# A hybrid decoder layer in split float32: the down projection and the last gate go token-major, half of their columns partly by Strassen's scheme

## The chip, the cores and the metric

The kernel runs on one core of one Trainium2 chip. The metric is the device time of one execution in microseconds (us). Before the change the median of three runs is 1440.21 us (1440.0 to 1440.61). The profile is one further execution of the same program; its first instruction and its last lie 1438.4 us apart (the span).

## The reference: what is computed

One layer over 256 tokens of width 2048, all in float32:

```
u  = rmsnorm(h);  proj = u @ w_in            # q, k, v of 16 heads and two gates
ya = dilated_mixture_attention(...) @ w_branch_a
yb = stick_breaking_attention(...) @ w_branch_b
h  = h + rmsnorm((sigmoid(ga) * ya + sigmoid(gb) * yb) @ w_out, g_mix_post)
u  = rmsnorm(h, g_ffn_pre)
up = causal_depthwise_conv(u @ w_up, conv_w, conv_b)       # 2 x 5632 columns
f  = (gelu(gate_ff) * value) @ w_down                       # 5632 -> 2048
h  = h + rmsnorm(f, g_ffn_post)
e  = p @ w_ple_in
h  = h + sigmoid(h @ w_ple_gate) * e
```

The change touches the last five lines from the product with `w_down` on, and where `h` and `e` are kept.

## The kernel before, in words

**Precision.** TensorE takes its operands as float32r, a rounded float32. Each operand x is therefore kept as two rounded parts, hi = round(x) and lo = round(x - hi), and each product is made of three: hi hi, hi lo and lo hi. For the weights ACT makes hi (L200) and DVE makes lo (L237) from the raw tile that a DMA brought.

**The weight stream.** The list `_plan()` gives the order in which blocks of 128 x 128 weights are used. Eight blocks make an item of 128 x 1024, 512 KB. There are 5 raw buffers (`NRAW`) and 7 pairs of split buffers (`NSPL`). `block()` hands PE the next block; at each eighth it calls `tick`, which writes the work of the other engines into their queues: first the ACT part of the deferred jobs that are due, then the hi of items up to six ahead, then DVE's lo of items that got their hi at an earlier tick, then the DVE part of the deferred jobs. `defer` hands in a job as a list of stages, and at each tick one more job starts and each running one goes on by a stage. Every engine works through its queue in the written order. Loads stand in SP's queue and are written by `lows` as raw buffers come free.

**Two ways to multiply.** By channel (`mul`, L318 and L320): the weights are the stationary operand and the activations the moving one; per block one matmul of 512 columns (hi against hi and lo of 256 tokens) and one of 256 columns (lo against hi), and the result stands with channels on the partitions. A last column group uses three of 256 (`mul1`, L338 to L340), so that no separate addition is left. By token (`three_wide`, L881, and `by_token`, L799 to L801): 128 tokens of the activation are stationary and 512 weight columns move, three matmuls for a half of the tokens, and the result stands with tokens on the partitions.

**Strassen's scheme before the change.** It is in use in `gate_groups` for the two gates of the first sub-layer, three column groups of four: the 2 x 2 blocks are token halves by k-tile pairs by two halves of 512 columns; seven products P1 to P7 take the place of eight. The sums of activation blocks are made once (`combine`), the sums of weight blocks (`weight_sums`, L210 and L211) for each group: the first in DRAM-to-SBUF transfers, a plain one and two that accumulate (`add_ahead`, issued by POOL, L224), the others on DVE. Such a pair of k-tiles is four items in the stream, of which two are sums.

**Residual and channel mixer.** `h` is kept by channel (`gh`). `turn` makes the post-norm of the mixer, adds to `h`, makes `u2`, and has the first half of `e` multiplied meanwhile (PE works on `e` while the norm's chain of small steps runs on DVE and ACT). Then come four quarters (`NQ`): 22 column tiles of `w_up` each (`up_evac`: two PSUM halves added, times the norm factor, the conv, gelu, product, split into `ft`), then 16 column tiles of `w_down` over the quarter's 11 rows of k-tiles, each added into `ff` (L379, L1170). After the last quarter a second `turn` makes the norm of `ff` (a ones-matmul sums squares over the partitions, L1035), the last `h` and its split `u3`, with the second half of `e`; then 16 column tiles of `w_ple_gate`, each with a sigmoid (L1194), a product with `e`, the addition of `h`, and a store of 128 KB.

Of the kernel before, what the change touches and what calls it, by code (L numbers as in the profile page):

```python
# [34 lines left out]
PAIRS = 4  # L35
SETTLE = dict(even=8, turned=9)
# [9 lines left out]
def _plan():  # L46
# [5 lines left out]
    def add(key, cols, nk, runs=None):  # L52
        plan.append((key, cols, runs or [list(range(nk))]))

# [15 lines left out]
    for j in range(0, KT, 4):  # L70
        gates = [[("w_in", o + kind * KT + n) for n in range(j, j + 4)] for kind in range(2)]
        if j == 0:
            add(("ga", j), gates[0], KT, single)
            add(("gb", j), gates[1], KT, single)
        else:

            order = [(4 * kind + c, k) for p in range(PAIRS) for kind, k in ((0, p), (1, p + 8), (0, p + 8), (1, p))
                     for c in range(4)]
            order += [(c, k) for k in _plain() for c in range(8)]
            plan.append((("gates", j), gates[0] + gates[1], order))  # L80
        add(("ba", j), [("w_branch_a", n) for n in range(j, j + 4)], NS, single[:NS])
        add(("bb", j), [("w_branch_b", n) for n in range(j, j + 4)], NS, single[:NS])
# [3 lines left out]
    add(("e", 0), [("w_ple_in", j) for j in range(8)], 2)  # L86
    up = [("w_up", half * NFF + n) for n in range(NFF) for half in range(2)]
    add("up", up[:FIRST], KT, single)
    for q in range(NQ):
# [3 lines left out]
        add(("down", q), [("w_down", j) for j in range(3)], 0, [rows[:-2], rows[-2:-1], rows[-1:]])  # L93
        for j in range(3, KT):
            add(("down", q, j), [("w_down", j)], 0, [rows])
    add(("e", 1), [("w_ple_in", j) for j in range(8, 16)], 2)
    add("pg", [("w_ple_gate", j) for j in range(FIRST)], KT, single)
    for j in range(FIRST, KT):
        add(("pg", j), [("w_ple_gate", j)], KT)
    return plan  # L100

# [13 lines left out]
def hybrid_block_kernel(ctx: ExitStack, tc: tile.TileContext, head, gx, pT, convp, bias, masks, w, out):  # L115
# [20 lines left out]
    stream, used, sums_of = [], 0, {}  # L136
    for g in _plan():
        if g[0][0] == "gates":
            assert used % 8 == 0
            while len(stream) < used // 8 + 2 * len(sums_of):  # L140
                stream.append(len(stream) - 2 * len(sums_of))
            for _ in range(PAIRS):
                i, r = len(stream), len(stream) - 2 * len(sums_of)
                stream += [r, None, None, r + 1]
                sums_of[i] = i + 3
        used += len(_order(g))
# [4 lines left out]
    part = {b for b in sums_of.values()}  # L151
    place = {r: i for i, r in enumerate(stream) if r is not None}
# [10 lines left out]
    def load(i, a=0, b=1024):  # L163
        if i not in raw:
# [5 lines left out]
    for g in _plan():  # L170
        if g[0][0] == "e":
            assert first_block % 8 == 0
            lent += [place[first_block // 8], place[first_block // 8 + 1]]
# [28 lines left out]
    def weight_sums(i):  # L202
# [4 lines left out]
        if n == 1:  # L207
            x = mps["mp"].tile([128, 2, 512], F32, name="wsum")
            raw[i] = [x[:, 0], x[:, 1]]
            DVE.tensor_tensor(x[:, 0], raw[a + 1][0], w0[:, 512:], OP.add)  # L210
            DVE.tensor_tensor(x[:, 1], x[:, 0], w1[:, :512], OP.add)  # L211
        return raw[i]

    def add_ahead(*ms):


        firsts = sorted(sums_of)
        for m in ms:
            if m < len(firsts):
                i, k = firsts[m], (4, 12, 0, 8)[m % PAIRS]  # L220
                to = gh[:, G + k * T:G + (k + 4) * T]
                nc.sync.dma_start(to, w[stream[i] - NE])
                for c in (0, 512):
                    nc.gpsimd.dma_start(to[:, c:c + 512], w[stream[i] + 1 - NE][:, 512:], accum_op=OP.add)  # L224
                raw[i + 1] = [to[:, :512], to[:, 512:]]

    def low(i, a=0, b=1024, src=None):
        if i in sums:
# [3 lines left out]
            if sums[i][1]:  # L232
                add_ahead(sorted(sums_of).index(sums[i][0]) + PAIRS)
# [122 lines left out]
    def mm(key, src, fn=mul, ps=None, even=0, turned=None, mid=None):  # L356
# [4 lines left out]
        for n, (_, k, first, last) in enumerate(group(key)):  # L361
            if n == 3 and mid:
                mid()
# [27 lines left out]
    gh = keep.tile([128, 4 * KT + KT * T], F32, name="gh")  # L391
# [491 lines left out]
    def gate_groups(j, merged):  # L883
# [3 lines left out]
        P3 = pm.tile([128, 2 * T], F32, name="sum")  # L887
# [52 lines left out]
    for j in range(0, KT, 4):  # L940
        if j:
            ga, gb = gate_groups(j, merged)
        else:
            for kind in ("ga", "gb"):
# [3 lines left out]
                if kind == "ga":  # L948
# [5 lines left out]
                    banks["of"] = [(pm1, 4), (pm, 3)] * 3 + [(pm1, 4)]  # L954
# [69 lines left out]
    def turn(half, edst, src, gnext, dst, nxt):  # L1024
# [3 lines left out]
        pr = pm.tile([128, 2 * T], F32, name="sum")  # L1028
        pse = []
        for i, (n, k, first, last) in enumerate(group(("e", half))):  # L1030
            if n % 2 == 0 and first:
                pse.append(bank())
            mul1(pse[-1][:, n % 2 * T:(n % 2 + 1) * T], pTs[:, k], first and n % 2 == 0, last)
            if i == 3 + half:
                PE.matmul(pr[:, :T], f(ones), sq[:, 0], start=True, stop=True)  # L1035
        rstd(pr)
        pss = [bank() for _ in range(FIRST)]
        gn = [None if gnext is None else gain(gnext, k) for k in range(KT)]
# [22 lines left out]
        def keep_e(n):  # L1061
            ACT.activation(edst[:, 2 * n:2 * n + 2].rearrange("p a b -> p (a b)"), pse[n], AF.Copy)
# [18 lines left out]
        for c, k, first, last in group(nxt):  # L1081
# [18 lines left out]

    e0 = fp.tile([128, 8, T], F32, name="e0")
    pss = turn(0, e0, mix, 2, u2, "up")


    ff = keep.tile([128, KT, T], F32, name="ff", tag="acc")
    ft = fp.tile([128, QT, 2 * T], F32R, name="ft", tag="ft")
    cpad = [fp.tile([128, T + 2], F32, name=f"cpad{n}") for n in range(4)]
    for c in cpad:
        DVE.memset(c[:, 0:2], 0.0)
    conv = {}  # L1110

    def up_evac(n, ps):

        c = cpad[n % 4]
# [17 lines left out]
        if n % 2:  # L1132
            st.append((lambda: usplit(ft, t, a, low=False), lambda: ulow(ft, t, a)))
        defer(*st)

    keys = [("up", n) for n in range(2 * NFF)]
    def mid():
        total(pm.tile([128, 2 * T], F32, name="sum"), sp)
# [8 lines left out]
    for n in range(FIRST, FIRST + 2):  # L1147
        pss.append(mm(keys[n], u2))
    flush()
    sp = halves()  # L1150
    for q in range(NQ):
        for n in range(max(len(pss), q * 2 * QT), (q + 1) * 2 * QT):
            ps = mm(keys[n], u2, **dict(SETTLE, mid=mid) if n == len(pss) else {})
            up_evac(n, ps)
        if q == NQ - 1:
            u3 = keep.tile([128, KT, 2 * T], F32R, name="u3", tag="u")
            lend(1, u3)
        down = several(("down", q), 3, ft)
        if q == NQ - 1:
            ACT.preload_act_table_set(LNEXP)  # L1160
        for j in range(KT):
            if q == NQ - 1 and j == KT - 1:
                break
            ps = down[j] if j < 3 else mm(("down", q, j), ft)

            def then(sum_to, j=j, q=q):
                if q == 0:
                    sum_to(ff[:, j])
                else:
                    DVE.tensor_tensor(ff[:, j], ff[:, j], sum_to(temp()), OP.add)  # L1170
            defer(both(ps, then), *([squares(ff, j), scaled(ff, j, 3)] if q == NQ - 1 else []))
    ps = mm(("down", NQ - 1, KT - 1), ft, mul1)
    lows(at["high"])
    flush()
    DVE.tensor_tensor(ff[:, KT - 1], ff[:, KT - 1], ps[:, :T], OP.add)
    square_sum(ff[:, KT - 1])
    scaled(ff, KT - 1, 3)[0]()


    e1 = fp.tile([128, 8, T], F32, name="e1", tag="ft")  # L1180
    pss = turn(1, e1, ff, None, u3, "pg")
    ACT.preload_act_table(AF.Sigmoid)

    def pg_evac(j, ps, whole=False):
        s = temp()
        e = (e0 if j < 8 else e1)[:, j % 8]
        first = (None, None) if whole else both(ps, lambda sum_to: sum_to(s))

        def dve():
            DVE.tensor_tensor(s, s, e, OP.mult)  # L1190
            o = temp("t", 3)
            DVE.tensor_tensor(o, s, h[:, j], OP.add)
# [81 lines left out]
```

## Time and profile before

| what | value |
|---|---|
| median of three runs | 1440.21 us |
| range | 1440.0 to 1440.61 us |
| span of the profiled execution | 1438.4 us |
| time of a run outside the span (median less span) | 1.8 us |
| PE busy | 1433.0 us, 100% of the span |
| DVE busy | 1086.7 us, 76% |
| ACT busy | 839.4 us, 58% |
| DMA | 290.78 MB, mean 202 GB/s |

The stage boundaries, from the first matmul of each stage: first half of `e` at 599.3 us, `up` from 605.5 us, the four stretches of `down` from 728.1, 911.1, 1094.2 and 1277.2 us, the second half of `e` at 1338.4 us, the gate `pg` from 1344.5 us; the last matmul starts at 1433.8 us. A matmul's duration in the profile is longer than its distance to the next one, since matmuls overlap in the array: rates are read from stretches of time and counts, not from the mean duration.

### The profile page before, as it was taken

How to read it: one execution, taken by the hardware profiler on the slowest of the kernel's cores; microseconds unless marked ns; L12 is line 12 of the kernel's file. 1: busy time of each engine (PE TensorE's matmuls, PEld its weight loads, DVE VectorE, ACT ScalarE, POOL GpSimd, SP SyncE). 2: the span in 40 equal slices, each digit the busy share in tenths (PEclk: the TensorE clock that was granted, in tenths of full speed). 3: DMA queues.
4: the chain of work that ended last, by engine and by line, in shares of the span. 5: the costliest groups of instructions: out<-in, count | busy, mean ns of one | idle time of the engine just before them, and what ended most of it. 6: DMA issues, size and time to landing. Idle time of an engine off the chain costs nothing.

```text
span 1438.4 us, 21464 instructions
## 1 busy us (share of the span) xinstructions
PE 1433.0 (100%) x8052; PEld 1254.9 (87%) x8052; DVE 1086.7 (76%) x1645; ACT 839.4 (58%) x1282; POOL 21.7 (2%) x29
## 2 busy tenths in 40 slices
PE   9999999999999999999999999999999999999998
PEld 8888888888888888988888888888888888888987
DVE  7876666669889865799965788767887677878784
ACT  7665555566556655576654555545655455657562
POOL 0000000002110000000000000000000000000000
PEclk9999999999999999999999999999999999999999
DMA  7754746479986776555766566666566666667381
GB/s 283 270 169 160 248 146 214 146 251 271 315 256 226 251 235 204 175 167 186 230 190 189 186 192 189 194 189 188 189 191 191 192 188 192 189 191 213 109 271 51
DMA packets 83334, 290.78 MB, mean 202 GB/s; under 512 B 9248, under 2 KB 11680, under 8 KB 83104
## 3 DMA queue, kind: packets, MB, share of 16 engines
q1 hardware_dynamic: 79776, 283.13, 61.4%
q0 software_dynamic: 3456, 6.29, 2.5%
q8 instruction: 63, 1.03, 0.3%
q14 instruction: 39, 0.32, 0.1%
HBM read 287.29 MB, written 2.10 MB: 201 GB/s over the span
## 4 chain that ended last, share of the span: by engine, by line
PE 100%; DVE 0%; ACT 0%; issue 0%
PE mm L318 47%; PE mm L320 24%; PE mm L881 7%; PE mm L646 2%; PE mm L644 2%; PE mm L645 2%; PE mm L799 2%; PE mm L800 2%; PE mm L801 2%; PE sum L881 2%; PE mm L340 1%; PE mm L339 1%; PE mm L338 1%; PE S L318 0%; PE S L657 0%; PE po L657 0%
## 5 line engine op out<-in xcount | busy, mean ns | idle before, releaser
L237 DVE TENSOR_TENSOR lo<-raw,hi 128x1024 fp32r<-128x1024 f32 (+1 forms) x497 | 596.5, 1210 | 155.2 <-ACT hi L200 149.2
L318 PE MATMUL mm<-u,hi 128*128 128x512 f32 x2044 | 710.4, 392 | 0.0
L200 ACT ACTIVATE hi<-raw 128x1024 fp32r<-128x1024 f32 (+1 forms) x497 | 516.0, 1046 | 227.5 <-PE mm L318 163.2
L320 PE MATMUL mm<-u,lo 128*128 128x256 f32 x2032 | 569.1, 280 | 0.0
L318 PEld LDWEIGHTS mm<-u,hi 128*128 128x128 f32 x2044 | 381.6, 187 | 82.5
L320 PEld LDWEIGHTS mm<-u,lo 128*128 128x128 f32 x2032 | 384.0, 189 | 1.3 <-DVE lo L237 0.6
L318 PE MATMUL mm<-ft,hi 128*128 128x512 f32 x693 | 240.4, 391 | 0.0
L376 ACT ACTIVATE t<-mm 128x256 f32<-128x256 f32 x209 | 79.0, 378 | 197.3 <-PE mm L320 197.0
L320 PE MATMUL mm<-ft,lo 128*128 128x256 f32 x693 | 194.0, 280 | 0.0
L318 PEld LDWEIGHTS mm<-ft,hi 128*128 128x128 f32 x693 | 129.6, 187 | 28.4
L379 DVE TENSOR_TENSOR s<-mm,t 128x256 f32<-128x256 f32 x178 | 75.1, 422 | 96.2 <-ACT t L376 96.2
L320 PEld LDWEIGHTS mm<-ft,lo 128*128 128x128 f32 x693 | 131.0, 189 | 0.0
L318 PE MATMUL mm<-mg,hi 128*128 128x512 f32 x232 | 80.5, 392 | 0.0
L881 PE MATMUL mm<-hi,u 128*128 128x512 f32 x192 | 66.2, 391 | 0.0
L320 PE MATMUL mm<-mg,lo 128*128 128x256 f32 x230 | 64.4, 280 | 0.0
L1123 ACT ACTIVATE cv<-cpad,cw 128x256 f32<-128x256 f32 x88 | 52.7, 599 | 8.1 <-DVE cpad L1118 7.8
L318 PEld LDWEIGHTS mm<-mg,hi 128*128 128x128 f32 x232 | 43.3, 187 | 9.3
L644 PE MATMUL mm<-hi,u 128*128 128x512 f32 x128 | 50.9, 398 | 0.0
L646 PE MATMUL mm<-hi,u 128*128 128x512 f32 x128 | 50.0, 391 | 0.0
L645 PE MATMUL mm<-lo,u 128*128 128x512 f32 x128 | 49.9, 390 | 0.0
L1127 DVE SCALAR_TENSOR_TENSOR cv<-cpad,cw,cv 128x256 f32<-128x256 f32 x88 | 42.7, 485 | 3.1
L320 PEld LDWEIGHTS mm<-mg,lo 128*128 128x128 f32 x230 | 43.5, 189 | 0.1
(287 smaller groups left out, 1548.0 us busy)
## 6 DMA issues: line engine op xcount, KB each, us to landing
raw<-in_w SPq DMA_DIRECT2D x501, 512.0 KB, 3.6
gh<-in_w SPq DMA_DIRECT2D x12, 512.0 KB, 5.3
gh<-in_w POOLq DMA_DIRECT2D x24, 256.0 KB, 7.6
hd<-in_head SPq DMA_DIRECT2D x6, 576.0 KB, 8.1
gh<-in_gx SPq DMA_DIRECT2D x6, 512.0 KB, 4.7
bi<-in_bias SPq DMA_DIRECT2D x4, 576.0 KB, 4.7
out<-t SPq DMA_DIRECT2D x16, 128.0 KB, 3.8
gh<-in_gx SPq DMA_DIRECT2D x1, 1056.0 KB, 7.5
```

The source lines that it names most:

```text
L200: ACT.activation(hi[i][:, a:b], raw[i][:, a:b] if src is None else src, AF.Copy)
L237: DVE.tensor_tensor(lo[i][:, a:b], raw[i][:, a:b] if src is None else src, f(hi[i][:, a:b]), OP.subtract)
L318: PE.matmul(ps, wh, rhs, start=first, stop=last, skip_group_check=True)
L320: PE.matmul(ps[:, :T], wl, rhs[:, :T], start=False, stop=last, skip_group_check=True)
L376: ACT.activation(t1[0], ps[:, T:], AF.Copy)
L379: DVE.tensor_tensor(out, ps[:, :T], t1[0], OP.add)
L644: PE.matmul(pv[t], xh, wh, start=kt == 0, stop=False)
L645: PE.matmul(pv[t], xh, wl, start=False, stop=False)
L646: PE.matmul(pv[t], xl, wh, start=False, stop=kt == KT - 1)
L881: PE.matmul(ps, x[i], w[j], start=first and n == 0, stop=last and n == 2, skip_group_check=True)
L1123: ACT.activation(y, c[:, 2:], AF.Identity, scale=cw[:, n, 2:3], bias=cw[:, n, 3:4])
L1127: DVE.scalar_tensor_tensor(y, c[:, 0:T], cw[:, n, 0:1], y, op0=OP.mult, op1=OP.add)
```

## The change

`w_down` and `w_ple_gate` are multiplied by token. Of the 16 column tiles, eight (1024 columns) take part of their rows by Strassen's scheme: in `down` eight of the eleven rows of a quarter in four pairs, in `pg` eight of sixteen k-tiles in four pairs; the rest of these columns' rows is plain, and the other eight column tiles are two groups `four` of 512 columns. The first weight sum of pairs 0 and 3 is made by transfers ahead of time (`sum_early`), the other sums on DVE; for pairs with transferred sums only half of the second weight tile is loaded. The activation sums of the pairs (`parts`) are made in `up_evac`. `join` and `join_to` put the seven products together, `ends` adds the plain rows.

The residual goes to token order: `home` transposes `h` in four calls of eight transposes among the first `up` tiles into `hx`. The norm of `ff` then needs no ones-matmul: squares are summed along the free axis (`square_to`), and the gain comes as a full tile (`weigh`). `turn_back` transposes the new `h` to channel order in eight calls of four, for `u3`. Since `hx` takes its space, the first half of `e` goes to DRAM and comes back before `pg`. `e` is made by token in four groups, and the output is stored by token in larger pieces. Eight PSUM banks now form one ring of 4 + 4; the separate bank `sum` is gone.

```diff
+DROWS = 8
+DSUM = (0, 3)
...
+        plan.append((("pairs", "down", q), down[:8],
+                     paired([(rows[r], rows[r + 1]) for r in range(0, DROWS, 2)]) + whole(rows[DROWS:])))
+        for c in (8, 12):
+            add(("down", q, c), down[c:c + 4], 0, [[r] for r in rows])
...
+    add(("pg", 0), pg[:4], KT, single)
+    plan.append((("pairs", "pg"), pg[4:12],
+                 whole(range(2 * PAIRS, KT)) + paired([(2 * p, 2 * p + 1) for p in range(PAIRS)])))
+    add(("pg", 12), pg[12:], KT, single)
...
+            if n == 0 or a in by_dma:
+                x = mps["mp"].tile([128, 2, 512], F32, name="wsum", tag="wsum")
...
+            if n == 0:
+                DVE.tensor_tensor(x[0], w0[:, :512], w1[:, 512:], OP.add)
+                DVE.tensor_tensor(x[1], w0[:, 512:], w1[:, 512:], OP.add)
+            else:
+                DVE.tensor_tensor(x[0], raw[a + 1][0], w0[:, 512:], OP.add)
+                DVE.tensor_tensor(x[1], x[0], w1[:, :512], OP.add)
...
+        def sums():
+            y.append(tmp.tile([128, 4, H], F32, name="y4", tag="s2", bufs=2))
+            DVE.tensor_tensor(y[0][:, 0], k1[:, H:], k2[:, H:], OP.subtract)
...
+        for p, (k1, k2) in enumerate(pairs):
+            last = p == len(pairs) - 1
+            s = [[mixed[:, p, i, n] for i in range(2)] for n in range(4)]
+            w11, w22 = item()
+            add(1, cut(src, k1, 0), w11, last)
+            if last:
+                ACT.activation(p1_to, bk[1], AF.Copy)
+            add((0, 1), s[3], w22, last and first_plain)
+            q, t3 = item()
+            add(5, s[0], q, last)
+            add(7, s[2], t3, last)
+            t2, t4 = item()
+            add(6, s[1], t2, last)
+            add((1, 0), cut(src, k2, 1), t4, last and first_plain)
+            w21, _ = item()
+            add((0, 0), cut(src, k2, 0), w21, last and first_plain)
...
-        pss.append(mm(keys[n], u2))
+        pss.append(mm(keys[n], u2, mid={3: home(8 * (n - FIRST)), 11: home(8 * (n - FIRST) + 4)}))
...
+    for t in range(2):
+        to = ff[:, t, 3 * 512:]
+        DVE.tensor_tensor(to, to, ps[t], OP.add)
+        square_to(t, 3)
+        ACT.activation(ln[:, t], ss[:, t, 3:4], AF.Ln, scale=1.0 / D, bias=base[:, t])
+        ACT.activation(y1[:, t], ln[:, t], AF.Exp, scale=-0.5)
+    for t in range(2):
+        small(t)
+        apply(0, 256, [t])
...
+    pse = e_cols(1, lambda n: n == 6 and turn_back(0))
+    apply(256, 512)
+    turn_back(1)
...
+    keep_e(0)
+    keep_e(1)
+    high3(0)
+    low3(0)
+    high3(1)
+    low3(1)
+    keep_e(2)
+    weigh(0, 3)
+    weigh(1, 3)
+    sum_early(True)
+    apply(512, 1024)
...
+    for k in range(KT):
+        n = k // 2 + 2
+        if k % 2 == 0 and 1 < k and n - 1 < KT // 2:
+            turn_back(n - 1)
+            high3(n - 1)
+            low3(n - 1)
...
+            k in (2, 6) and apply(128 * (k + 6), 128 * (k + 6) + 512)
...
+    sigmoid(ps, 3, [0])
+    finish([(0, 1536, 2048)])
+    for a in (1536, 1792):
+        ACT.activation(ff[:, 1, a:a + 256], ps[1][:, a - 1536:a - 1536 + 256], AF.Sigmoid)
+        finish([(1, a, a + 256)])
```

`small(t)` is four operations on one column per partition, and `apply(a, b)` adds the normed `ff` to `hx` for columns a to b, one operation per token half. `e_cols` makes eight groups of three matmuls and calls its second argument after each.

## Prediction before the run

> **What bounds the kernel now.** The page's first part and its chain come first.
>
> ```profile
> span 1438.4 us, 21464 instructions
> PE 1433.0 (100%) x8052; PEld 1254.9 (87%) x8052; DVE 1086.7 (76%) x1645; ACT 839.4 (58%) x1282; POOL 21.7 (2%) x29
> PEclk9999999999999999999999999999999999999999
> PE 100%; DVE 0%; ACT 0%; issue 0%
> ```
>
> PE is never out of work and its clock is at full in all slices. So time falls only with PE's own work, and rises wherever another engine is late. To price PE's work I read stretches: one Strassen stretch of the first sub-layer, then every stage that changes.
>
> ```profile
> 404.31:423.35 19.04, 19.04 (x85) 15.77 (x85) 18.90 (x27) 13.01 (x19) 3.55 (x4) 1.00 0.89 247
> 599.30:605.50 6.20, 6.20 (x53) 6.14 (x52) 4.25 (x11) 3.31 (x7) 0.00 (x0) 1.00 0.29 91
> 728.10:789.10 61.00, 61.00 (x354) 53.78 (x353) 34.60 (x43) 29.37 (x41) 0.00 (x0) 1.00 0.63 192
> 789.10:911.10 122.00, 122.00 (x706) 107.57 (x705) 97.42 (x149) 71.48 (x107) 0.00 (x0) 1.00 0.62 189
> 911.10:972.10 61.00, 61.00 (x354) 53.78 (x353) 40.98 (x58) 29.37 (x41) 0.00 (x0) 1.00 0.61 192
> 1094.20:1155.20 61.00, 61.00 (x355) 53.78 (x354) 40.98 (x58) 29.36 (x41) 0.00 (x0) 1.00 0.61 191
> 1277.20:1338.35 61.15, 61.15 (x365) 54.38 (x364) 47.27 (x73) 43.21 (x74) 0.00 (x0) 1.00 0.68 207
> 1338.35:1344.55 6.20, 6.20 (x53) 6.12 (x51) 4.23 (x11) 3.68 (x7) 0.00 (x0) 1.00 0.27 93
> 1344.55:1434.10 89.55, 89.53 (x554) 80.44 (x552) 62.16 (x102) 43.20 (x74) 0.00 (x0) 1.00 0.46 146
> ```
>
> The columns are the length, then the busy time and count of PE, PE's weight loads, DVE, ACT and POOL, the clock, and DMA. A quarter of `down` is 176 blocks in 61.00 us: 0.3466 us a block by channel (a matmul of 512 columns and one of 256). The chain in order of time gives the rate by token, and that of transposes.
>
> ```profile
> 362.62 4.08 PE mm L881 x18
> ...
> 384.38 0.87 PE mm L824 x8
> 385.25 0.69 PE mm L881 x3
> 385.95 0.68 PE sum L881 x3
> ```
>
> Eighteen matmuls of 512 columns take 4.08 us: 0.2267 us each, so a block by token (six for four blocks) is 0.340 us. The two ways are almost equal: 0.0066 us a block. Who reads the mean durations (392 and 280 ns) as costs would expect 13%; they overlap. What is left is Strassen's eighth product.
>
> [...]
>
> **The change on PE.** Each quarter of `down` is now four pairs of 7 x 3 matmuls, three plain rows of 12, and two `four` groups of 11 x 6: 84 + 36 + 132 = 252, at 0.2267 us 57.1 us. Four quarters: 228.5 us for 244.15, **-15.65**. `pg`: 84 + 8 x 12 + 2 x 96 = 372 matmuls, 84.3 us for 89.55, **-5.2**. `e`: 24 matmuls a half, 5.44 us; the first half keeps its ones-matmul (0.4 us, what 48 matmuls of 256 columns at 0.3466 - 0.2267 = 0.12 us leave of the 6.20): 5.84 for 6.20, the second 5.44 for 6.20: **-1.1**. Added are 64 transposes in 12 calls: 0.87 / 8 = 0.109 us each, and next to nothing for the hand back to matmuls (from 385.25 to 385.95 three of them take 0.70 for 0.68): **+7.0**. PE's balance is **-14.95 us**.
>
> **DVE in the pair stretches.** This is the first place to lose it. In the row 404.31:423.35 DVE has 18.90 of 19.04 us: a pair costs DVE more than PE.
>
> ```profile
> 408.67 1.82 DVE L237 TENSOR_TENSOR lo<-raw,hi 128x512 fp32r<-128x512 f32 x2
> 410.41 0.69 DVE L210 TENSOR_TENSOR wsum<-gh,raw 128x512 f32<-128x512 f32 x1
> 411.13 0.69 DVE L211 TENSOR_TENSOR wsum<-wsum,raw 128x512 f32<-128x512 f32 x1
> 411.74 1.29 DVE L231 TENSOR_TENSOR lo<-gh,hi 128x512 fp32r<-128x512 f32 x2
> 412.94 1.29 DVE L231 TENSOR_TENSOR lo<-wsum,hi 128x512 fp32r<-128x512 f32 x2
> 414.15 1.82 DVE L237 TENSOR_TENSOR lo<-raw,hi 128x512 fp32r<-128x512 f32 x2
> ```
>
> From 408.67 to 414.15 is one pair: 5.48 us of DVE against 4.76 of PE. Pairs 1 and 2 have their first sums on DVE too, two more additions at 0.605 us (half of the 1.21 between 411.74 and 412.94): 6.7 us. Four pairs are 24.4 us, and 2.5 us of the last `up` tile's steps (two PSUM sums, the norm factor, the conv, the product, the split) fall among them: 26.9 against 19.04. What covers the difference is DVE's lead. In `up` it is the full six items:
>
> ```profile
> ACT hi L200 <- PE mm L318: 13.2, 22, 1.3
> DVE lo L237 <- ACT hi L200: 3.2, 12, 1.2
> ```
>
> These are the waits of 1155.2 to 1277.2 us: for 22 of 44 items ACT waits until PE frees a split buffer, so the seven are full. Six items of a pair stretch are the first pair, a raw tile and the next first sum: 5.48 + 1.14 + 2.4 = 9.0 us, so 17.9 stay. PE reaches the lo of the last pair's second sum 3 x 4.76 + 13 x 0.2267 = 17.2 us after the start, and of the 17.9 the second half of this sum and the last half tile (0.6 each) may come later: 16.7, 0.5 us in hand. DVE waits for ACT's hi behind each of its own sums, about 0.4 us a pair. I take **+0.5 us** a quarter, +2.0 in all; the bounds are 0 and 2 a quarter. `pg` has eight plain items ahead of its pairs and no `up` steps in them: 0.
>
> `up` pays for `parts`, four pairs a quarter of four operations on 128 elements and one on 512: 4 x 4 x 0.29 + 4 x 0.69 = 7.4 us.
>
> ```profile
> L859 DVE TENSOR_TENSOR comb<-comb x4: 291/292/295, 319.3 to 334.1; 128x128 f32<-128x128 f32 x4
> 705.00:728.00 23.00, 23.00 (x135) 20.25 (x134) 19.92 (x32) 13.80 (x21) 0.00 (x0) 1.00 0.70 214
> ```
>
> In a later quarter DVE has 97.4 of 122 us, so this is hidden. In the first it is full up to 705 us and has 3.1 us left at the end; the PE time that `home` adds there (32 transposes, 3.5 us) and these carry 6.6 of the 7.4. I cost it at nothing; the lead is what would suffer.
>
> **Around the last norm.** Count from the end T of the last `down` matmul's issue.
>
> ```profile
> 1338.56 0.42 DVE L1175 TENSOR_TENSOR ff<-ff,mm 128x256 f32<-128x256 f32 x1 [0.35 <-PE mm L340]
> L443 ACT ACTIVATE s<-gh x11: 612/620/636, 23.5 to 631.8; 128x512 f32<-128x512 f32 x11
> L685 ACT ACTIVATION_READ_ACCUMULATOR e<-e,st x8: 184/187/188, 69.9 to 279.1; 128x1 f32 x8
> L686 DVE RECIPROCAL st<-st x8: 163/164/166, 70.2 to 279.3; 128x1 f32<-128x1 f32 x8
> L1127 DVE SCALAR_TENSOR_TENSOR cv<-cpad,cw,cv 128x256 f32<-128x256 f32 x88 | 42.7, 485 | 3.1
> L913 DVE SCALAR_TENSOR_TENSOR ga<-mm,Rc,ga 128x512 f32<-128x512 f32 x6 | 4.2, 745 | 0.0
> ```
>
> DVE starts 0.2 us after PE's last (1338.36 to 1338.56). The second half's addition ends at T + 0.9, its square with the accumulator read at 1.75, Ln and Exp on one column (0.19 to 0.42; I take 0.25) at 2.25, four column operations at 0.2 at 3.1, `apply` of 256 columns at 3.6. `turn_back(0)` stands after six groups of `e`, at 4.1: not late. `apply(256, 512)` ends at 4.5, `turn_back(1)` stands at 5.44 + 0.44 = 5.9 and `pg` begins at 6.3. But DVE's next `apply` stands behind `low3(1)`, which needs `turn_back(1)` (6.3), its latency (0.25) and ACT's copy (0.6): 7.15 to 7.85; then two gain products (1.2) and two `apply` of 512 (1.4) end at 10.5, while PE stands at `turn_back(2)` from 6.3 + 12 x 0.2267 = 9.0. PE waits **1.5 us**. From there each two k-tiles take PE 3.16 us with their transposes, and DVE at most 0.6 + 1.4 + 1.14: no more waits. Bounds: 0 (were DVE's order covered) and 4.
>
> **The tail.**
>
> ```profile
> 1434.12 0.38 ACT L1194 ACTIVATE s<-mm 128x256 f32<-128x256 f32 x1 [4.39 <-PE mm L340]
> 1434.54 0.43 DVE L1190 TENSOR_TENSOR s<-s,e 128x256 f32<-128x256 f32 x1 [3.88 <-ACT s L1194]
> 1435.00 0.43 DVE L1192 TENSOR_TENSOR t<-s,gh 128x256 f32<-128x256 f32 x1
> ```
>
> Before, the last store is issued 1.5 us after PE's end and the span ends 3 us later. After, the first token half's 512 columns keep DVE until 0.9, then two pieces of 256 take four steps, to 2.55: **+1.1** (0.4 to 2).
>
> **Hidden.** The store of `e` to DRAM must land before `home` overwrites `hx`; its issue stands in SP's queue behind loads that DVE frees some 5 us before that, and a transfer of its size took 7.5 us. ACT may wait a microsecond with six items in hand: 0 (up to 4, when a bank is late for the next `home`). DMA moves 247 GB/s in the old pair stretch without holding PE; here pairs 1 and 2 load 1 MB in 4.76 us, 220 GB/s.
>
> **The sum.** -14.95 + 2.0 + 1.5 + 1.1 = -10.35 us: span 1428.0 us, and with the 1.8 us that lie around it in the median, **1429.9 us**.
>
> **Rivals.** *All of it is hidden*: no wait in the pairs, none at the norm, a tail of +0.4: -14.5, 1425.7 us. For it: the old pair stretches have the same kind of deficit and PE has no gap in them. Against it: the order of `low3(1)` and `apply`.
>
> *The pair stretches begin without the lead.* If DVE is three items ahead and not six at their start (raw tile and two sums, 4.9 us of work done instead of 9), each quarter stalls 4.1 us more: +16.4, **1446 us**, slower. The point is where four stalls pass 14.95 - 2.6 = 12.3 us, 3.1 each, a lead between three and four items. For it: DVE is full from 645 to 705 us (19.5 of each 20), and `parts` loads `up` further. Against it: 24.6 us idle in a later quarter.
>
> *Transposes do not overlap.* At their whole duration of 273 ns 64 cost 10.5 us more: 1440 us, no change. For it only the duration; against it 0.87 us for eight, at full clock.
>
> ```profile
> L824 PE MATMUL mm<-idt,gb x32: 270/273/273, 384.2 to 514.4; 128*128 128x128 f32 x32
> ```
>
> [...]
>
> *Each `turn_back` waits for its own copy and split.* A wait of 1 us at the six in `pg`: +6, 1436 us, near the edge of what shows.
>
> **How the numbers follow.** The forecast has 0.56 (its own range 1426.5 to 1434), all hidden 0.12, the lead lost 0.13, transposes 0.05, the waits at `turn_back` 0.14. A measurement of this kernel tells about 0.2% (2.9 us) from no change. Faster is the first two and half of the last: 0.75; same is the transposes and the other half: 0.12; slower 0.13. The range is 1425.5 to 1440: it leaves out the lead lost and the transposes, 0.18.
>
> **What will show it.** Right: `down` stretches of 57 to 58 us, 1.5 us of PE idle ahead of the third `turn_back`, transposes 0.11 us apart, ACT still waiting for PE at the end of `up`. Wrong: `down` stretches over 59.5 us with PE waiting for DVE's lo of a sum, or a clock below full near transposes.

## The result and the profile after

The changed kernel takes 1454.6 us in the median (1453.56 to 1455.18), against 1440.14 us before in the same comparison: a ratio of 1.0098, 95% interval 1.0084 to 1.0113. It is slower by 1.0%; 1429.9 us was forecast. The profiled execution spans 1452.5 us. The page after, its head, the clock and the chain of work that ended last:

```profile
span 1452.5 us, 20479 instructions
PE 1433.1 (99%) x7475; PEld 1221.6 (84%) x7475; DVE 1166.5 (80%) x1785; ACT 860.3 (59%) x1295; POOL 39.4 (3%) x49
...
PE 92%; DVE 3%; DMA 2%; ACT 1%; issue 1%; ACTq 0%; DVEq 0%
```

PE has 577 matmuls fewer and is as long busy as before (1433.1 for 1433.0 us). So there are two losses: PE waits, and its matmuls have become slower somewhere. The busy times by stage show both (columns as in the prediction):

```profile
605.20:731.36 126.16, 126.16 (x764) 112.60 (x764) 116.72 (x211) 85.98 (x146) 1.75 (x2) 1.00 0.55 181
731.36:796.00 64.64, 59.73 (x254) 46.65 (x253) 51.91 (x68) 36.77 (x48) 3.54 (x4) 1.00 0.74 233
796.00:920.40 124.40, 124.40 (x706) 107.86 (x705) 103.53 (x175) 73.13 (x114) 1.78 (x2) 1.00 0.57 180
920.40:979.50 59.10, 57.96 (x255) 47.07 (x254) 50.48 (x65) 32.44 (x40) 1.78 (x2) 1.00 0.70 236
...
1287.70:1346.30 58.60, 57.90 (x254) 47.03 (x254) 53.26 (x72) 36.30 (x53) 0.00 (x0) 1.00 0.69 237
1346.30:1352.50 6.20, 6.20 (x32) 5.14 (x31) 3.93 (x14) 4.32 (x12) 0.00 (x0) 1.00 0.52 184
1352.50:1447.40 94.90, 89.70 (x399) 73.16 (x397) 77.61 (x110) 50.21 (x68) 3.54 (x4) 0.98 0.52 166
```

PE's waits of the whole execution (total, times, longest, in us):

```profile
PE mm L927 <- DVE ff L1285: 3.8, 1, 3.8
PE mm L927 <- DVE x L1296: 2.8, 3, 1.3
PE mm L927 <- DVE lo L283: 2.6, 3, 1.4
PE mm L927 <- DVE lo L275: 1.5, 6, 0.5
PE mm L1437 <- DVE hx L1411: 1.4, 2, 1.0
PE mm L927 <- DVE ff L1286: 1.3, 1, 1.3
```

Stage lengths, each from the first matmul of a stage to the first of the next (us); the tail begins 0.23 us after the start of the last matmul. "Mended" and "best" are the fourth and the seventh experiment below.

| stage | before | after | mended | best |
|---|---|---|---|---|
| `up` of quarter 1 | 122.63 | 126.18 | 126.18 | 126.17 |
| `up` of quarters 2, 3, 4, each | 122.03 | 124.36 | 122.15 | 122.15 |
| `down` of quarter 1 | 61.01 | 64.65 | 63.03 | 59.88 |
| `down` of quarters 2, 3, 4 | 61.01, 61.01, 61.15 | 59.09, 59.45, 58.63 | 58.40, 58.44, 58.41 | 58.39 each |
| second half of `e` | 6.18 | 6.27 | 6.27 | 6.27 |
| `pg` | 89.50 | 94.83 | 88.41 | 88.38 |
| tail | 4.36 | 5.14 | 5.36 | 5.26 |
| span | 1438.4 | 1452.5 | 1436.5 | 1432.8 |

The step from 1438.4 to 1452.5 is +14.1 us. PE's own work gives -14.95, as the prediction has it. Against that stand: `up` of three quarters, 3 x 2.33 = +7.0, with PE busy all the time; `down` above its 57.1 us of matmuls, 7.5 + 2.0 + 2.3 + 1.5 = +13.3; `pg` above 84.3 us and 24 transposes (2.6), +7.9; the tail +0.8. The sum is +14.0.

Three suspicions came out of this. A: after a stretch by token the blocks by channel run in a slower rhythm. B: the first quarter's pairs meet DVE without its lead, because ACT waited 4.6 us for the store of `e`. C: PSUM banks that the groups `four` need are set free late, since `join` and `join_to` stand in DVE's queue behind up to six lo's of later items.

### The profile page after: what moved, and what is told of

The parts are those of the page before. It is cut to its first block, busy times and chain, and to the rows that moved or that the text cites. A ratio compares the mean times of both kernels' runs of the same rounds, so it can differ in the third digit from the quotient of the medians.

```text
span 1452.5 us, 20479 instructions
## 1 busy us (share of the span) xinstructions
PE 1433.1 (99%) x7475; PEld 1221.6 (84%) x7475; DVE 1166.5 (80%) x1785; ACT 860.3 (59%) x1295; POOL 39.4 (3%) x49
## 3 DMA queue, kind: packets, MB, share of 16 engines
q1 hardware_dynamic: 80752, 285.76, 58.4%
## 4 chain that ended last, share of the span: by engine, by line
PE 92%; DVE 3%; DMA 2%; ACT 1%; issue 1%; ACTq 0%; DVEq 0%
PE mm L364 33%; PE mm L927 25%; PE mm L366 17%; PE mm L692 2%; PE mm L690 2%; PE mm L691 2%; PE mm L845 2%; PE mm L847 2%; PE mm L846 2%; DMA raw<-in_w 2%; DVE lo L283 1%; ACT hi L228 1%; DVE lo L275 1%; PE S L364 0%; PE S L703 0%
## 5 line engine op out<-in xcount | busy, mean ns | idle before, releaser
L283 DVE TENSOR_TENSOR lo<-raw,hi 128x1024 fp32r<-128x1024 f32 (+1 forms) x497 | 581.9, 1187 | 115.3 <-ACT hi L228 110.7
L364 PE MATMUL mm<-u,hi 128*128 128x512 f32 x1828 | 643.2, 396 | 0.0
L366 PE MATMUL mm<-u,lo 128*128 128x256 f32 x1818 | 509.9, 281 | 0.0
L927 PE MATMUL mm<-hi,ft 128*128 128x512 f32 x544 | 172.4, 391 | 4.1 <-DVE x L1296 2.8
L927 PEld LDWEIGHTS mm<-hi,ft 128*128 128x128 f32 x544 | 102.1, 188 | 27.3 <-DVE x L1296 4.0
L927 PE MATMUL mm<-lo,ft 128*128 128x512 f32 x272 | 106.8, 393 | 2.6 <-DVE lo L283 2.6
L927 PEld LDWEIGHTS mm<-hi,u 128*128 128x128 f32 x456 | 86.4, 190 | 22.1 <-DVE ff L1285 4.3
L224 ACT ACTIVATE hi<-wsum 128x512 fp32r<-128x512 f32 x84 | 51.1, 630 | 49.2 <-DVE wsum L247 38.9
L927 PEld LDWEIGHTS mm<-lo,ft 128*128 128x128 f32 x272 | 51.0, 188 | 15.1 <-DVE lo L283 4.8
L275 DVE TENSOR_TENSOR lo<-wsum,hi 128x512 fp32r<-128x512 f32 x84 | 54.3, 685 | 0.3
L927 PE MATMUL mm<-hi,mixed 128*128 128x512 f32 x160 | 52.8, 391 | 0.0
```

Of the source, the lines that this page charges most:

```text
L224: ACT.activation(hi[i][:, n * 512:(n + 1) * 512], x, AF.Copy)
L275: DVE.tensor_tensor(lo[i][:, to], x, f(hi[i][:, to]), OP.subtract)
L283: DVE.tensor_tensor(lo[i][:, a:b], raw[i][:, a:b] if src is None else src, f(hi[i][:, a:b]), OP.subtract)
L364: PE.matmul(ps, wh, rhs, start=first, stop=last, skip_group_check=True)
L366: PE.matmul(ps[:, :T], wl, rhs[:, :T], start=False, stop=last, skip_group_check=True)
L927: PE.matmul(ps, x[i], w[j], start=first and n == 0, stop=last and n == 2, skip_group_check=True)
```

## Experiments

**1. The rhythm.** The first `up` tile of quarters 2 to 4 starts with eight blocks of three 256-column matmuls and the order of the ninth turned, as one tile of the first quarter already does (`SETTLE`).

```diff
-            ps = mm(keys[n], u2, **dict(SETTLE, mid={3: mid}) if n == len(pss) else {})
+            ps = mm(keys[n], u2, **dict(SETTLE, mid={3: mid}) if n == len(pss) else SETTLE if q and n == q * 2 * QT else {})
```

> In the changed kernel a block by channel takes 353.3 ns in the up stretches of quarters 2 to 4 and 346.7 ns in the first (124.36 us against 122 us a stretch). Theory A: PE has two rhythms for the pair of 512 and 256 columns, the switch from matmuls by token leaves it in the slow one, and the eight blocks of three matmuls with one block in turned order, which the first up tile of the first quarter has, put it into the fast one. Given to the first up tile of quarters 2 to 4, the three stretches take 122.1 us each and the span falls by 6.8 us, from 1452.5 to about 1445.7. Rival: the stretches are slow because of where operands lie or because of DVE and DMA traffic; then they stay at 124.4 and the span at 1452.5.

Measured: 1449.33 us, ratio 1.0062 (1.0047 to 1.0077), span 1447.3. The second and the third quarter's `up`:

```profile
796.30:918.40 122.10, 122.10 (x713) 107.98 (x712) 103.30 (x175) 73.15 (x114) 1.78 (x2) 1.00 0.60 184
...
978.00:1100.10 122.10, 122.10 (x713) 107.98 (x712) 104.10 (x177) 72.65 (x113) 1.77 (x2) 1.00 0.60 184
```

In the changed kernel the same stage had 706 matmuls in 124.40 us, here it has seven more in 122.10, at the same clock of 1.00 and with no wait in either. 352 blocks: 353 ns each against 347. A is right for the changed kernel: the slow rhythm lasts the whole stage, and eight blocks in another form, with a ninth in turned order, end it. The span fell by 5.2 us and not by 6.8: the three `up` gave 6.6, but `pg` took 95.86 us for 94.83, and the granted clock of the whole execution was 0.994 for 0.999 (run 3 shows the changed kernel's spell at a lower clock).

**2. The store of `e`.** The half of `hx` that `home` overwrites first is no longer the one whose store is under way.

```diff
-    pss = turn(hx[:, :, :D // 2], mix, u2)
+    pss = turn(hx[:, :, D // 2:], mix, u2)
...
-    nc.sync.dma_start(e0, hx[:, :, :D // 2])
+    nc.sync.dma_start(e0, hx[:, :, D // 2:])
```

> The first half of e is put into the right half of hx ahead of its store to DRAM, so the first two calls of home write the left half and wait for no store. Theory B: in the changed kernel ACT's copy waits 4.6 us for that store, DVE idles 4.7 us for want of ACT's hi, and this is the lead that the first quarter's pair stretch lacks: the first down stretch (64.65 us) falls to 59 to 60.5, the span by 4 to 6 us to 1447 to 1448.5. Rival: the lead is lost to DVE's own work (the added parts on top of a full engine) or to the 2 MB of transfers beside the weights; then the stretch stays at 63 us or more and the span within 1.5 us of 1452.5.

Measured: 1454.3 us, 1.0093 (1.0078 to 1.0109), span 1452.2. Waits of 620 to 660 us, first in the changed kernel, then here:

```profile
DVE lo L283 <- ACT hi L228: 4.7, 1, 4.7
ACT hx L1233 <- DMA e<-hx: 4.6, 1, 4.6
```

```profile
ACT hx L1233 <- PE mm L1232: 3.4, 2, 3.1
DVE lo L283 <- ACT hi L228: 3.3, 1, 3.3
```

The wait for the store is gone, and ACT's copies, written ahead of the next hi, wait for their transposes instead: DVE's wait shrinks from 4.7 us to 3.3 and doesn't go. The first `down` takes 64.39 us for 64.65. So the store is not the cause that B took it for. That the 3.3 us of waiting left aren't the cause either is seen only in run 8: its DVE waits 3.4 us at the same place, and its first `down` takes 57.88 us.

**3. The joins.** In `down`, `join` and `join_to` are written when the pairs are, ahead of the lo's of the following items. In `pg` the join stood there already; its four last additions (`ends`) go to a later tick. In both, no lo's are written while the last products of the last pair are issued (`hold`, in `pg` two products earlier).

```diff
+            at["hold"] = last and hold_at == 1
             q, t3 = item()
             add(5, s[0], q, last)
             add(7, s[2], t3, last)
+            at["hold"] = last
             t2, t4 = item()
...
-        defer((None, (lambda bk=bk, o=o: join(o, bk)) if q == 0 else lambda bk=bk, o=o, x=x: join_to(o, bk, x)))
+        join(o, bk) if q == 0 else join_to(o, bk, x)
+        at["hold"] = False
...
-    ends(o, bk)
+    at["hold"] = False
+    defer((None, lambda: ends(o, bk)))
```

> Splitting of later weights is held back during the last pair, and the joining of the seven products is written ahead of it into DVE's queue (in pg the last four additions go to a later tick). Theory C: the next group of four waits for PSUM banks that the joining frees, and the joining stands behind three to five lo operations and their loads. Then PE's waits at the start of the groups of four (1.5, 1.2, 1.5 and 0.8 us in down, 4.0 us and 1.6 us at half clock behind it in pg) fall to about 0.5 us each, and the span by 6 to 8 us to 1444.5 to 1446.5. Rival: DVE is simply out of time there; then the waits move to the lo of the plain rows and the span stays within 2 us of 1452.5.

What the joins stood behind in `pg`, in DVE's timeline of the changed kernel (start, length):

```profile
1417.30 6.60 DVE L283 TENSOR_TENSOR lo<-raw,hi 128x512 fp32r<-128x512 f32 x6
1423.82 0.68 DVE L1285 TENSOR_TENSOR ff<-mm,ff 128x512 f32<-128x512 f32 x1
```

and PE's, at the first matmul of the second half of tokens in group `four`, which needs the bank that L1285 reads:

```profile
1420.34 0.39 PE L927 MATMUL mm<-hi,u 128*128 128x512 f32 x1
1424.56 0.50 PE L927 MATMUL mm<-hi,u 128*128 128x512 f32 x1 [3.83 <-DVE ff L1285]
```

After this wait the clock falls:

```profile
1420.00:1429.00 9.00, 5.17 (x16) 3.79 (x15) 8.78 (x13) 3.77 (x5) 0.00 (x0) 0.81 0.56 216
```

From 1425.4 to 1428.8 us it is 0.50, and 0.19 x 9 / 0.5 = 3.4 us is what the 0.81 over 9 us comes to; an estimated 1.7 us more is lost by it. With the edit: 1445.66 us, 1.004 (1.0026 to 1.0055), span 1443.9; `pg` 89.64 us at a clock of 1.00, `down` 63.13 and three times 58.3. The row of `pg`, and two rows of PE's waits:

```profile
1348.90:1438.50 89.60, 88.04 (x399) 71.94 (x397) 77.45 (x110) 50.31 (x68) 3.54 (x4) 1.00 0.57 176
```

```profile
PE mm L927 <- DVE lo L283: 3.2, 6, 1.4
PE mm L927 <- DVE ff L1287: 0.2, 1, 0.2
```

C is right: 5.2 us in `pg` and 1.5 + 0.8 + 1.2 + 0.3 in the four stretches of `down`. Of 7.9 us of waits for joins (L1285, L1286, L1296) 0.2 are left, and those for lo's of L283 grew by 0.6 only.

**4. All three together**, and `apply(512, 1024)` written ahead of the two gain products (`weigh`) for the third `turn_back`.

> The three edits together, and the gain products of the last columns moved behind the application of columns 512 to 1023, so that the third turn_back waits 1.2 us less. If theories A, B and C hold and add up: 1452.5 - 6.8 - 5 - 7 - 1.2 = 1432.5 us of span, 1434.3 us of time, faster than before the change. If only A holds, 1445.

Measured: 1437.54 us, 0.9983 (0.9974 to 0.9993), span 1436.5: the stages of the column "mended". That is 4.0 us above the theory with all three, chiefly since the 5 us of B didn't come. The change is now worth a little less than what can be told from none; the largest loss left is in the first `down`.

**5. The order by token alone**, without the scheme: no parts, no weight sums, no joins, every group a `four`. The edit in the plan of `down` (that of `pg` is alike):

```diff
-        plan.append((("pairs", "down", q), down[:8],
-                     paired([(rows[r], rows[r + 1]) for r in range(0, DROWS, 2)]) + whole(rows[DROWS:])))
-        for c in (8, 12):
+        for c in (0, 4, 8, 12):
```

> Only the order is changed, not the scheme: all of down and of the ple gate goes by token in plain groups of four blocks, nothing by Strassen's scheme, no differences of the activations, no weight sums, no joins. Theory (the pair stretches and their joins are what stalls): the four down stages take 176 x 340 ns = 59.8 us each and the ple gate 1.6 to 5.6 us of waits less and 2.7 us more of matmuls than in the changed kernel, about 92 us; the up stages of quarters 2 to 4 stay at 124.36 us (the slow rhythm has nothing to do with the scheme); span about 1447. Rival (the order by token itself outruns VectorE, which has to split the weights faster): the first down stage stays above 63 us and the span at 1460 or more.

Measured: 1454.66 us, 1.0098 (1.0082 to 1.0115), span 1452.5: 5.5 us over the theory, and not for its reason. `down` takes 59.87 to 59.88 us four times and `up` 124.36, as expected, `pg` 91.34; but the second half of `e` takes 12.08 for 6.27 us. ACT from 1344 to 1352.5 us:

```profile
L1408 ACT ACT_TABLE_LOAD x2 | 2.6, 1283 | 0.0
L1409 ACT ACT_TABLE_LOAD x2 | 2.6, 1283 | 0.0
```

The edit had put the load of the table for Ln and Exp ahead of the last gelus, so that ACT loaded tables four times in the norm's chain: 5.1 us, a fault of the experiment. Run 10 repeats it without that.

**6. The same rhythm in the kernel before?** The constant serves two tiles of that kernel, one in the first `up` and one in `pg`, and the edit takes the setting out of both.

```diff
-SETTLE = dict(even=8, turned=9)
+SETTLE = dict()
```

> The kernel before, with only the rhythm-setting start of one up tile taken out (the tile is run like every other). Theory (after a stretch of equal matmuls the alternation of 512 and 256 columns falls into a slow rhythm of 353.3 ns a block and stays there until it is set right): all later blocks by channel, about 2000 of them in up, down and the ple gate, cost 6.7 ns more each, span about 1438.4 + 13 = 1451; up 124.4 us and down 62.2 us in each quarter. Rival 1 (the rhythm rights itself at the next tile or stage): only the first up stage is longer, by 2 us at most, span 1440. Rival 2 (no such rhythm): 1438.4 as before.

Measured: 1439.9 us, 0.9998 (0.9989 to 1.0008), span 1438.7. The rest of the first `up`, the second `up` and the second `down`:

```profile
640.00:728.60 88.60, 88.60 (x514) 78.20 (x514) 82.04 (x141) 59.54 (x97) 0.00 (x0) 1.00 0.65 200
789.60:911.60 122.00, 122.00 (x706) 107.67 (x705) 97.39 (x149) 71.42 (x107) 0.00 (x0) 1.00 0.61 190
911.60:972.60 61.00, 61.00 (x354) 53.83 (x353) 40.96 (x58) 29.32 (x41) 0.00 (x0) 1.00 0.62 192
```

122.00 us with the same 706 matmuls that take 124.40 in the changed kernel. My theory for this run falls: the old kernel needs no setting. Its later `up` follow on blocks by channel, which may be the reason; no run shows it. What brings the slow rhythm about is open; a stretch by token ahead is not the only way, since the kernel before has most of it in a row of its own, soon after its start (159 matmuls in 28.0 us, 352 ns a block):

```profile
12.00:40.00 28.00, 27.96 (x159) 24.05 (x158) 23.98 (x38) 22.70 (x38) 0.00 (x0) 1.00 0.76 279
```

**7. The first quarter without the scheme**, on the mended kernel.

```diff
-        plan.append((("pairs", "down", q), down[:8],
-                     paired([(rows[r], rows[r + 1]) for r in range(0, DROWS, 2)]) + whole(rows[DROWS:])))
-        for c in (8, 12):
+        if q:
+            plan.append((("pairs", "down", q), down[:8],
+                         paired([(rows[r], rows[r + 1]) for r in range(0, DROWS, 2)]) + whole(rows[DROWS:])))
+        for c in (8, 12) if q else (0, 4, 8, 12):
...
-            paired = t % 2 and t < DROWS
+            paired = n >= 2 * QT and t % 2 and t < DROWS
```

> The mended kernel (rhythm set at each quarter, residual stored from its other half, joins issued at once, weigh after apply: span 1436.5, first down stage 63.03) with the first quarter's down wholly by token without the scheme; the other quarters and the ple gate as they are. Theory D (the scheme costs the first quarter its 5 us because its lead is not back when the pairs and their sums come): first down stage 176 x 340 ns = 59.84 us, at most 60.5; span 1433.3 to 1434. Theory E (the lead is lost to the residual's turning and its copies on ScalarE, and any order by token meets it empty): the first down stage stays at 61.5 to 63.5, span 1435 to 1437.

Measured: 1434.85 us, 0.9961 (0.9946 to 0.9976), span 1432.8. PE is never idle in the first `down`:

```profile
731.30:791.20 59.90, 59.90 (x266) 49.65 (x265) 29.36 (x28) 28.34 (x33) 0.00 (x0) 1.00 0.62 194
913.40:971.80 58.40, 57.94 (x255) 47.03 (x254) 50.41 (x65) 32.44 (x40) 1.75 (x2) 1.00 0.73 237
```

E is refuted: without the scheme PE never waits in this stage, though `home` and its copies stand ahead of it as before. So the loss is the scheme's, as D has it (which part of it, run 8 asks), and this is the best version met: 0.39% faster than the kernel before. The scheme pays 1.5 us in a later quarter (59.88 to 58.39) and lost 3.2 in the first.

**8. The pairs without their parts**, first quarter only.

```diff
-            paired = t % 2 and t < DROWS
+            paired = n >= 2 * QT and t % 2 and t < DROWS
...
+            if key[-1] == 0:
+                s = [cut(src, (k1, k2)[n // 2], n % 2) for n in range(4)]
```

> The mended kernel with the differences of the activations (the parts: four subtractions, a rounding and a low half for each pair) left out in the first quarter only; its pair stretch keeps its matmuls, its weight sums and its loads, and reads the halves of the activations in place of the differences, so the first quarter's result is not the reference's. Theory D1 (the parts' 7.4 us of VectorE in a quarter whose VectorE is full are what the first down stage lacks): first down stage 58.4 us as in the other quarters, span 1431.9. Theory D2 (the pair stretch itself, its sums and its loads of 2 MB, needs more lead than the first quarter has by then): first down stage 61.5 to 63, span 1435 to 1436.5.

Measured: span 1430.4, time 1432.3 us, 0.9945 (0.993 to 0.996), first `down` 57.88, half a microsecond below the expectation. The row of that stage here, then in the mended kernel:

```profile
731.10:789.00 57.90, 57.63 (x254) 47.12 (x254) 46.81 (x58) 33.90 (x43) 1.75 (x2) 1.00 0.74 241
```

```profile
731.70:794.70 63.00, 59.35 (x254) 46.72 (x253) 51.92 (x68) 36.74 (x48) 3.54 (x4) 1.00 0.73 237
```

DVE has 5.1 us less left to do in that stage, and the stage is 5.1 us shorter. D1 is right in this: it is the parts, not the pair stretch with its sums and its 2 MB, that the first quarter can't carry. The parts have work for ACT too, which has 2.8 us less in the stage; this run alone doesn't tell the two engines apart.

**9. The parts' subtractions on GpSimd**, first quarter only (`e` is an argument of `parts`; all four of its first operations change alike).

```diff
-            DVE.tensor_tensor(y[0][:, 0], k1[:, H:], k2[:, H:], OP.subtract)
...
+            e.tensor_tensor(y[0][:, 0], k1[:, H:], k2[:, H:], OP.subtract)
...
-            sums, high, low = parts(t // 2, conv[n - 3], a) if paired else (None, None, None)
+            sums, high, low = parts(t // 2, conv[n - 3], a, DVE if n >= 2 * QT else nc.gpsimd) if paired else (None, None, None)
```

> The mended kernel with the four subtractions of the first quarter's parts moved from VectorE to GpSimd, which does nothing between its two sum loads at 633 and 732 us; their rounding (ScalarE) and low halves (VectorE, 4 x 0.68 us) stay. Theory D1 narrowed (it is VectorE's time that the parts take, 4.6 of 7.3 us of it in these subtractions): the first down stage falls from 63.03 towards 57.9, about (63.03 - 57.88) x 4.6 / 7.3 = 3.2 us, to 59.8; span 1433.3. Rival D3 (the parts cost the lead through ScalarE, whose rounding waits for them in order, or VectorE and GpSimd hinder each other): the first down stage stays at 62.5 or more, span 1436 or more, and the mean time of VectorE's instructions between 645 and 725 us is longer than before.

Measured: 1436.54 us, 0.9974 (0.9964 to 0.9984), span 1434.5, first `down` 61.88: 1.15 us gained where 3.2 were expected. DVE's costliest group of 640 to 725 us in the mended kernel and here, and GpSimd's slowest:

```profile
L283 DVE TENSOR_TENSOR lo<-raw,hi 128x1024 fp32r<-128x1024 f32 x30 | 36.3, 1219 | 0.0
...
L1184 DVE TENSOR_TENSOR y<-cv 128x128 f32<-128x128 f32 x4 | 1.1, 284 | 0.0
```

```profile
L283 DVE TENSOR_TENSOR lo<-raw,hi 128x1024 fp32r<-128x1024 f32 x30 | 37.4, 1254 | 0.0
...
L1184 POOL TENSOR_TENSOR y<-cv 128x128 f32<-128x128 f32 x4 | 3.8, 950 | 0.0
```

The lo's are 35 ns longer (1.1 us in all) while GpSimd takes 950 ns for what takes DVE 284. Three more groups of DVE grew in the same 85 us (`ft` of L465 from 419 to 537 ns, `cpad` of L1200 from 426 to 461, `cv` of L1208 from 479 to 500); with the lo's that makes 3.2 us, so of the 4.6 us taken off DVE 1.4 remain, and the stage gained 1.15. Why DVE's groups take longer here no run shows. The second part of the miss is the clock, here and in the mended kernel:

```profile
738.00:748.00 10.00, 8.00 (x27) 5.69 (x26) 9.84 (x17) 5.92 (x10) 0.00 (x0) 0.83 0.29 96
```

```profile
738.00:748.00 10.00, 7.16 (x28) 4.61 (x27) 9.80 (x18) 5.82 (x11) 0.00 (x0) 1.00 0.27 80
```

PE waits less here, 2.0 of these 10 us against 2.8, and gives part of it back at the lower clock, 0.83 for 1.00. So the test doesn't separate the engines cleanly. That it is DVE's time and not ACT's is argued from the sizes (5.1 us in run 8, about 1.4 here) and from ACT's waits, which in the end of the first `up` are for DVE (the rows follow in the next section); no run takes only ACT's share out.

**10. By token alone, mended**: run 5 with the rhythm, the store, the order of `weigh`, and the table loaded behind the gelus.

> All by token and nothing by the scheme, as in the run of the order alone, but with the rhythm set at each quarter, the residual stored from its other half, weigh after apply, and the table of Ln and Exp loaded after the last gelu (in the run before it stood ahead of them, and four table loads of 1.28 us followed in the norm). Theory: down 59.87 four times, up of quarters 2 to 4 122.15, the second e stage 6.3, the ple gate 88.4 + 2.7 = 91.1 us; span 1452.5 - 6.6 - 5.8 = 1440.1, so the order by token alone is no gain over 1438.4 and the scheme in three quarters and the gate gives the rest: 1440.1 against 1432.8. Rival (the scheme's stages were carried by something else, the rhythm or the order): span 1434 or less.

Measured: 1440.66 us, 1.0004 (0.9995 to 1.0014), span 1438.4 (first `down`, second `up`, `pg`):

```profile
730.90:790.80 59.90, 59.90 (x267) 49.57 (x266) 29.37 (x28) 28.34 (x33) 0.00 (x0) 1.00 0.63 194
790.80:912.90 122.10, 122.10 (x713) 107.98 (x712) 96.97 (x148) 71.64 (x107) 0.00 (x0) 1.00 0.60 190
1343.20:1433.30 90.10, 90.10 (x410) 74.23 (x408) 52.67 (x57) 39.83 (x46) 0.00 (x0) 1.00 0.46 158
```

PE is busy throughout and the order by token alone brings nothing: `down` gains 4.7 us (61.01 to 59.88 in each quarter) and the gate's matmuls 2.0 (90.13 less 2.6 of transposes, for 89.50), the 64 transposes take 7.0. The scheme gives what there is to gain: 1438.4 to 1432.8 with it in three quarters and the gate.

## Why the prediction was wrong, by its own steps

**PE's balance** was right. 252 matmuls at 0.2267 us are 57.1; the first quarter without its parts came to 57.88 with waits in it, and by token alone 59.88 was measured for 264 x 0.2267 = 59.85. The 32 transposes among `up` took 126.18 - 122.63 = 3.55 us for 3.5; the rival of transposes that don't overlap is refuted. The second `e` with eight of them is 6.27 for 6.31. By token 176 blocks went from 61.01 to 59.88 us, 6.4 ns a block for the 6.6 that were forecast.

**`up` after a stretch by token** failed by omission: "The two ways are almost equal" took the rate by channel from stretches of the kernel before, where no stretch by token stands ahead of `up`, and no term allowed for another rate, though the row of 12 to 40 us shown under run 6 had it. It cost 7.0 us.

**DVE in the pair stretches.** For quarters 2 to 4 the wait was forecast in its right size: 0.5 us a quarter, and PE's waits for lo's in `down` are 1.4 us in three quarters of the best version:

```profile
PE mm L928 <- DVE lo L276: 0.8, 3, 0.3
PE mm L928 <- DVE lo L284: 0.6, 3, 0.2
```

A wait costs more than its row, though: in the second quarter of this version the two of 0.28 and 0.18 us put the matmuls off by 0.56 and 0.45, and in that of the changed kernel one of 0.18 us put them off by 0.46. The first quarter is where the step failed: "I cost it at nothing; the lead is what would suffer". The lead was read from a wait row of 1155 to 1277 us, three quarters later. The end of the first `up` in the kernel before (690 to 728 us), the same in the changed one (690 to 731), and its second quarter (878 to 920):

```profile
ACT hi L200 <- PE mm L318: 2.0, 4, 0.7
```

```profile
ACT cv L1205 <- DVE cpad L1200: 6.6, 8, 1.5
ACT ft L459 <- DVE cv L1211: 5.3, 5, 1.5
```

```profile
ACT t L422 <- PE mm L366: 10.8, 7, 1.9
...
ACT hi L228 <- PE mm L364: 3.0, 6, 0.7
```

Before, and in the second quarter, ACT has waits for PE to free split buffers (the rows of hi): the lead is full. In the first quarter of the changed kernel all its waits are for DVE. The rival "the pair stretches begin without the lead" named the mechanism; it happened in one quarter and not in four. Its price of 4.1 us stands against 4.6 measured, 63.03 less 58.4 of the other quarters in the mended kernel; how many items of lead were left wasn't measured, so that the sizes are near may be luck. The 7.4 us of parts were rightly summed; that 6.6 of them were carried was wrong, since the 3.1 us in hand before came at the very end of the stage, where, by the first of these rows, the lead was full again; that the stage lost because this refilling no longer took place is inferred from the rows, and that the parts are its cause is shown by run 8.

**No wait was listed for PSUM banks.** The change puts 4 + 4 banks into a ring and each `four` takes banks that a join has to read first. I priced DVE's load in the stretches and not the place of the joins in its queue. It cost 5.2 us in `pg`, 1.7 of them by the clock, and 3.8 us in `down` (run 3).

**Around the last norm** the step was right: 1.5 us at the third `turn_back` forecast, 1.4 in the row of waits (1.8 with the handing over). With `apply` ahead of the gain products 0.3 us are left, so the cause was DVE's order, as given. The rival of a wait at each `turn_back` is refuted: the other five show none.

**The tail** was +0.8 for +1.1. **Hidden**, the store of `e`: ACT did wait 4.6 us, and 0 was right for PE: without that wait run 2 is no faster beyond the scatter of its runs.

The forecast's span of 1428.0 was short by 24.5 us: the rhythm 7.0, the first quarter's pairs 4.6, the joins 3.8 + 5.2, and 0.8 in each `down` that stays in the mended kernel (58.4 for 57.1 + 0.5; in the second quarter about 0.5 of it is what the waits cost beyond their rows, the rest isn't traced) 3.2; 0.7 are not traced either. The rival "all of it is hidden" is refuted with these. The range ended at 1440 and left the lead lost (1446) outside; each rival had one cause, and here three causes came together.

## What to carry to other kernels

Read the lead of an engine that runs ahead from the stretch in which it will be used, and not from a later turn of the same loop: work that is hidden in turns 2 to 4 can stand on the path in turn 1. Where a change lets more stages share PSUM banks, find for each bank the instruction that frees it and what is written ahead of it in that engine's queue. And after a change in the form of the matmuls compare time per matmul in the stages that were not touched.

## What the runs showed of the hardware that was not expected

An alternation of matmuls of 512 and 256 columns has two rates at the same clock of 1.00 and with no wait: 347 and 353 ns a block (122.1 and 124.4 us for a stage of 352 blocks). Behind a stretch of 512-column matmuls it kept to the slower one for 352 blocks (124.40 us, the changed kernel); a start in another form cured it (122.10 us, run 1), and behind blocks of its own form it was fast without that (122.00 us, run 6).

The clock fell to 0.50 for 3.4 us after a wait of 3.83 us (rows of the changed kernel under run 3), but it fell also in the first `down` of runs 9 and 1. Run 9's longest wait for a lo of this stage is 1.4 us, and the mended kernel, whose longest is 1.4 us too, kept its clock at the same place. The rows of waits of run 9 and of the mended kernel, then the stretches of run 9, run 1 and the mended kernel:

```profile
PE mm L927 <- DVE lo L283: 1.9, 2, 1.4
```

```profile
PE mm L927 <- DVE lo L283: 2.6, 3, 1.4
```

```profile
740.00:745.00 5.00, 3.00 (x8) 1.65 (x7) 5.00 (x9) 2.52 (x4) 0.00 (x0) 0.81 0.30 105
745.00:750.00 5.00, 5.00 (x20) 4.03 (x19) 4.73 (x7) 3.77 (x6) 0.00 (x0) 0.85 0.48 126
```

```profile
740.00:745.00 5.00, 2.90 (x9) 1.53 (x9) 4.93 (x9) 3.07 (x6) 0.00 (x0) 0.96 0.23 72
745.00:750.00 5.00, 4.72 (x11) 3.75 (x12) 4.73 (x9) 2.84 (x5) 0.00 (x0) 0.50 0.42 142
750.00:755.00 5.00, 5.00 (x20) 3.97 (x20) 4.96 (x8) 4.04 (x7) 0.00 (x0) 0.86 0.32 120
```

```profile
740.00:745.00 5.00, 2.89 (x9) 1.53 (x9) 4.93 (x10) 3.13 (x6) 0.00 (x0) 1.00 0.23 61
745.00:750.00 5.00, 4.45 (x18) 3.32 (x19) 4.73 (x9) 2.79 (x5) 0.00 (x0) 1.00 0.43 148
```

Taken at 0.50, these rows make an estimated (0.19 + 0.15) x 5 / 0.5 = 3.4 us of lower clock in run 9 and (0.04 + 0.50 + 0.14) x 5 / 0.5 = 6.8 us in run 1. From 740 to 745 us PE is busy 2.90 us in run 1 and 2.89 in the mended kernel, and behind it the clock is 0.50 in run 1 and 1.00 in the mended kernel. So the length of one wait doesn't tell here whether the clock falls; what does, no run shows.
